# Seven block products instead of eight in half of a projection's contraction, in a two-layer attention trunk on one core

## The chip, the cores and the metric

One core of one Trainium2 chip. The metric is device time in microseconds (us) of one execution; lower is better. Engines are named as in the profile: PE (matrix products), DVE (VectorE), ACT (ScalarE), POOL (GpSimd) and SP (SyncE, which issues all the DMAs here).

## The reference

Two layers run one after the other on x of 256 tokens by 2048 features, all in float32: layer A (latent attention) and layer B (differential attention). The change touches layer B's input projection, `z = rms_norm(x, norm_g) @ w_in`, which is cut to this:

```python
z = rms_norm(x, norm_g) @ w_in                    # (256, 2048) @ (2048, 8192)
q, k, v, gate = split(z)                          # 2048 columns each, 8 heads
q = rms_norm(q.reshape(b, s, 8, 2, 128), q_gain)  # two maps a head; k likewise
o = diff_attend(q, k, v, pos, lam)                # softmax map 1 - lam * softmax map 2, times v (256 wide)
return x + (rms_norm(o, subln_g) * c * silu(gate)) @ w_out
```

## The kernel before

**Split products.** Each float32 operand of a product is split into a high part `hi` (rounded to the PE's format) and a low part `lo = x - hi`. `mm3` (L122 to L125) then makes one product of three matmuls: hi·hi, hi·lo, lo·hi. Weights are streamed: `stream` (L105) loads a chunk of 128 partitions x 1024 float32 (512 KB) into `raw` (four buffers), ACT writes `whi` (L118) and DVE writes `wlo` (L119), each of which has three buffers. A chunk holds two contraction tiles (`kk`) of 128 rows, each 512 columns wide.

**Layer B.** Each of the 8 heads has 1024 columns of the projection: a block of 512 for q and k (`wB[2h]`, summed in the two PSUM banks `pg`, one for each half `t` of the tokens) and a block of 512 for v and gate (`wB[2h+1]`, banks `pu`). `project` (L127) goes through the 8 chunks of a block: 8 x 2 `kk` x 2 `t` x 3 = 96 matmuls of 512 columns, so 192 a head. The loop over heads (L745 to L758) interleaves the attention steps of head h between pieces of these projections: `qk_t` (transposes of q and k), `soft_b` (scores and softmax), `p_b`, `av_b`, `go_b`. After the qk block, `qk_b` squares it on ACT, POOL takes the reciprocal root (`fb`, L92), and DVE multiplies from PSUM into `qk` (L641). `vg_b` splits v from PSUM (`vhb`, `vlb`) and makes the gate `sgb` (L668, L669).

**What sets the order.** Every engine has one queue in order; the tile library adds the waits and places instructions by a schedule of its own. SP's queue holds all loads. A tile with one buffer can be written again only after its last reader.

Of the kernel before, what the change touches and what calls it, by code (L numbers as in the profile page):

```python
# [51 lines left out]


@with_exitstack
def hybrid_kernel(ctx: ExitStack, tc: tile.TileContext, x, xT, pos, posc, rows, gains, wz, wgA, wqu, wkvu, woA, wB, woB, out):
# [105 lines left out]
    sqx = sm.tile([P, 2 * S], F32, tag="kn", name="sqx", bufs=1)  # L161
    XC = [0, 1] + list(range(2, KD + 1, 2))
    for k in range(KD):
        def load_x(k=k):
            n = XC[XC.index(k) + 1] - k
            xs = att.tile([P, n, S], F32, tag="gT", name="xs", padded_shape=[P, 4, S])
            nc.sync.dma_start(xs, xT[:, k:k + n, :])
            if k == 0:
                nc.sync.dma_start(gains_t, gains)
            xt[0] = (k, xs, n)  # L170

        if k in XC and k > 0:
            load_x()
        wh, wl = stream(wz[k], ZW, [c for c, _ in ZB] + [ZW] if k < KCUT else None, load_x if k == 0 else None)
        k0, xs, n = xt[0]
        split_gain(xh[:, k, :], xl[:, k, :], xs[:, k - k0, :], gA_t[:, k:k + 1])
        for b, (c0, w) in enumerate(ZB):
            for t in range(NT):
                sl = slice(t * P, (t + 1) * P)
                mm3(zacc[b][t][:, :w], xh[:, k, sl], xl[:, k, sl], wh[:, c0:c0 + w], wl[:, c0:c0 + w],  # L180
                    k == 0, k == KD - 1)
        if k == k0 + n - 1:
            w = n * S
            if k < 2:
                A.activation(sqx[:, k * S:(k + 1) * S], xs.rearrange("p a b -> p (a b)"), AF.Square)
            else:
                sq = sm.tile([P, w], F32, tag="sg", name="sq", bufs=2)
                A.activation(sq, xs.rearrange("p a b -> p (a b)"), AF.Square)
                G.tensor_tensor(sqx[:, :w], sqx[:, :w], sq, ALU.add)
# [46 lines left out]
    cs = sm.tile([P, 2, NT, HR], F32, tag="cs", name="cs", bufs=1)  # L236
# [9 lines left out]
    ropc = const.tile([P, 2, NT, ROPE], F32, tag="ropc", name="ropc")  # L246
    rops = const.tile([P, 2, NT, ROPE], F32, tag="rops", name="rops")
# [20 lines left out]
    maskA = const.tile([P, NT, S], F32, tag="maskA", name="maskA")  # L268
# [8 lines left out]
    # lambda, on every partition  # L277
# [8 lines left out]
    m16 = big.tile([P, 2, 2, 4, S], F32R, tag="m16", name="m16")  # L286
    krope = const.tile([P, NT, ROPE], F32, tag="krope", name="krope")
# [4 lines left out]
    def latents():  # L292
# [13 lines left out]
        for t in range(NT):  # L306
            cn = att.tile([P, 2, LORA], F32, tag="gT", name="cn")
# [86 lines left out]
    def q_up(hp):  # L394
        """queries of two heads, not scaled: their norm enters with the scores"""
# [4 lines left out]
        r2 = sm.tile([P, NT, 2, ROPE], F32, tag="r2", name="r2", bufs=1)  # L400
# [21 lines left out]
    def head_t(hp):  # L422
# [179 lines left out]
    def mm_b(i, pool, c0, c1):  # L602
        if c0 == 0:
            state["acc", i] = pair(pool)
        project([state["acc", i]], lhs1, [wB[i]], 512, c0, c1, KD)
        if c1 == KC:
            return state.pop(("acc", i))

    mm_b(0, psg, 0, 2)
# [17 lines left out]
    def qk_b(h, c0, c1):  # L627
        acc = mm_b(2 * h, psg, c0, c1)
        if not acc:
            return  # L630
# [9 lines left out]
        for t in range(NT):  # L640
            V.tensor_tensor(qk[:, t], acc[t].rearrange("p (j d) -> p j d", j=4), bc(f[:, t], HD), ALU.mult)  # L641
# [16 lines left out]
    def vg_b(h, c0, c1):  # L658
        acc = mm_b(2 * h + 1, psu, c0, c1)
        if not acc:  # L660
            return
# [77 lines left out]
    def out_b(n, pool, c0, c1):  # L739
        if c0 == 0:  # L740
            oacc[n] = pair(pool)
        project([oacc[n]], feat(goh2, gol2), [woB[n]], 512, c0, c1, KD)

    qk_b(0, 2, KC)
    for h in range(BH):  # L745
        vg_b(h, 0, 3)
        qk_t(h)
        vg_b(h, 3, 5)
        soft_b(h)
        vg_b(h, 5, 7)  # L750
        p_b(h)
        vg_b(h, 7, KC)
        nxt = (lambda a, b: qk_b(h + 1, a, b)) if h + 1 < BH else (lambda a, b: out_b(0, psg, a, b))
        nxt(0, 2)
        av_b(h)
        nxt(2, 5)
        go_b(h)
        nxt(5, KC if h + 1 < BH else 7)  # L758

# [22 lines left out]
def _columns(w, width):  # L782
    """(K, N) -> (N / width, K / 256, 128, 2 * width): blocks of columns in chunks of two row tiles."""
# [49 lines left out]
```

## Time and profile before

| | |
|---|---|
| median of 3 runs (lowest to highest) | 847.49 us (846.46 to 847.53) |
| span of the profiled execution | 845.0 us |
| PE, DVE, ACT, POOL busy | 99%, 67%, 58%, 10% of the span |
| bytes read from HBM | 145.73 MB |
| period of a head of layer B | 48.3 us |

The time of the profiled execution itself is not listed apart from its span; the median of the three runs is 2.5 us above that span, and these 2.5 us lie around the span (start and end of the program). The profile's views are of this one execution. In them a line such as L119 is a line of the kernel above; a row of the timeline gives start and duration in us.

### The profile page before, as it was taken

Reading aid. Unit: us, or ns where it says so; the run is one execution under the profiler, and the core shown is the slowest. Engines: PE = TensorE matmul, PEld = TensorE weight load, DVE = VectorE, ACT = ScalarE, POOL = GpSimd, SP = SyncE. Lnnn points to the kernel's source line nnn. Section 1 sums busy time; section 2 is a strip of 40 time slices with the busy share of each in tenths; the row PEclk is TensorE's granted clock in tenths of the full one; section 3 lists DMA queues with packets and bytes.
Section 4 is the critical chain, followed back from the end, with each engine's and each line's share of the span. In section 5 each row is a group of like instructions: output and inputs, shape, how many; then the busy total and the mean of one; then the engine's idle time right before and its main releaser. Section 6 shows DMA issues by size and latency. Waiting matters only on the chain.

```text
span 845.0 us, 11706 instructions
## 1 busy us (share of the span) xinstructions
PE 835.9 (99%) x4187; PEld 714.5 (85%) x4187; DVE 564.6 (67%) x968; ACT 488.0 (58%) x995; POOL 86.4 (10%) x113
## 2 busy tenths in 40 slices
PE   8999999999999999999999999999999999999998
PEld 6988888889888888888888888888888888888886
DVE  6968678788787866555647565565756566565543
ACT  7656687677767656555555465555555564554331
POOL 2300221122202200000010010010001000000000
PEclk9999999999999999999999999999999999999999
DMA  8755544534444645555555555554555555455661
GB/s 268 256 197 162 166 147 146 176 116 162 144 144 149 248 154 180 180 186 177 185 175 174 175 175 175 175 175 150 193 181 175 175 175 171 168 184 198 219 211 70
DMA packets 42954, 148.59 MB, mean 176 GB/s; under 512 B 5008, under 2 KB 6032, under 8 KB 42640
## 3 DMA queue, kind: packets, MB, share of 16 engines
q1 hardware_dynamic: 42896, 147.84, 52.5%
q8 instruction: 33, 0.54, 0.3%
q14 instruction: 25, 0.20, 0.1%
HBM read 145.73 MB, written 2.10 MB: 175 GB/s over the span
## 4 chain that ended last, share of the span: by engine, by line
PE 94%; DVE 3%; DMA 1%; ACT 1%; issue 0%; SPq 0%; POOL 0%; DVEq 0%; ACTq 0%
PE pu L123 14%; PE pu L125 14%; PE pu L124 14%; PE pg L124 13%; PE pg L123 13%; PE pg L125 13%; DVE wlo L119 1%; PE ptb L651 1%; PE ptn L430 1%; PE ptp L484 1%; PE pa L124 1%; DMA raw<-in_wz 1%; PE pa L125 1%; PE pa L123 1%; DVE xl L152 1%; PE ps L462 0%
## 5 line engine op out<-in xcount | busy, mean ns | idle before, releaser
L119 DVE TENSOR_TENSOR wlo<-raw,whi 128x1024 fp32r<-128x1024 f32 (+4 forms) x278 | 328.6, 1191 | 189.8 <-ACT whi L118 189.5
L118 ACT CAST whi<-raw 128x1024 fp32r<-128x1024 f32 (+3 forms) x277 | 282.2, 1025 | 233.6 <-PE pg L125 102.6
L123 PE MATMUL pu<-whi,x1h 128*128 128x512 f32 x256 | 101.3, 396 | 0.0
L123 PE MATMUL pg<-whi,x1h 128*128 128x512 f32 x256 | 100.5, 392 | 0.0
L125 PE MATMUL pu<-whi,x1l 128*128 128x512 f32 x256 | 99.9, 390 | 0.0
L124 PE MATMUL pu<-wlo,x1h 128*128 128x512 f32 x256 | 99.8, 390 | 0.0
L124 PE MATMUL pg<-wlo,x1h 128*128 128x512 f32 x256 | 99.7, 390 | 0.0
L125 PE MATMUL pg<-whi,x1l 128*128 128x512 f32 x256 | 99.7, 389 | 0.0
L125 PEld LDWEIGHTS pu<-whi,x1l 128*128 128x128 f32 x256 | 48.1, 188 | 10.2
L125 PEld LDWEIGHTS pg<-whi,x1l 128*128 128x128 f32 x256 | 48.1, 188 | 10.1
L123 PEld LDWEIGHTS pg<-whi,x1h 128*128 128x128 f32 x256 | 48.1, 188 | 9.5
L124 PEld LDWEIGHTS pg<-wlo,x1h 128*128 128x128 f32 x256 | 48.1, 188 | 9.4
L124 PEld LDWEIGHTS pu<-wlo,x1h 128*128 128x128 f32 x256 | 48.2, 188 | 9.2
L123 PEld LDWEIGHTS pu<-whi,x1h 128*128 128x128 f32 x256 | 48.1, 188 | 9.2
L123 PE MATMUL pg<-whi,xh 128*128 128x512 f32 (+1 forms) x128 | 49.8, 391 | 1.9 <-ACT whi L118 1.3
L124 PE MATMUL pg<-wlo,xh 128*128 128x512 f32 (+1 forms) x128 | 48.7, 381 | 1.9 <-DVE wlo L119 1.9
L123 PE MATMUL pg<-whi,goh 128*128 128x512 f32 x128 | 50.5, 395 | 0.0
L123 PE MATMUL pu<-whi,goh 128*128 128x512 f32 x128 | 50.1, 392 | 0.0
L124 PE MATMUL pg<-wlo,goh 128*128 128x512 f32 x128 | 49.9, 390 | 0.0
L125 PE MATMUL pg<-whi,gol 128*128 128x512 f32 x128 | 49.9, 390 | 0.0
L124 PE MATMUL pu<-wlo,goh 128*128 128x512 f32 x128 | 49.9, 390 | 0.0
L125 PE MATMUL pu<-whi,gol 128*128 128x512 f32 x128 | 49.9, 389 | 0.0
(246 smaller groups left out, 1551.1 us busy)
## 6 DMA issues: line engine op xcount, KB each, us to landing
raw<-in_wB SPq DMA_DIRECT2D x128, 512.0 KB, 3.2
raw<-in_wgA SPq DMA_DIRECT2D x32, 512.0 KB, 3.5
raw<-in_woA SPq DMA_DIRECT2D x32, 512.0 KB, 3.3
raw<-in_woB SPq DMA_DIRECT2D x32, 512.0 KB, 3.2
raw<-in_wkvu SPq DMA_DIRECT2D x16, 512.0 KB, 4.3
raw<-in_wz SPq DMA_DIRECT2D x15, 544.0 KB, 5.7
raw<-in_wqu SPq DMA_DIRECT2D x16, 384.0 KB, 3.1
x<-in_x SPq DMA_DIRECT2D x1, 2048.0 KB, 10.0
```

What stands on the lines that cost most here:

```text
L118: (V.tensor_copy if after_first and a == 0 else A.copy)(hi[:, a:b], raw[:, a:b])
L119: V.tensor_tensor(lo[:, a:b], raw[:, a:b], f32(hi[:, a:b]), ALU.subtract)
L123: T.matmul(o, shi, mhi, start=start, stop=False)
L124: T.matmul(o, shi, mlo, start=False, stop=False)
L125: T.matmul(o, slo, mhi, start=False, stop=stop)
L152: V.scalar_tensor_tensor(lo, src, g, f32(hi), ALU.mult, ALU.subtract)
L430: T.transpose(pt[:, h, t * P:(t + 1) * P], src[:, t, h, :NOPE], ident)
L484: T.transpose(pt[:, c, t * P:(t + 1) * P], e[:, t, c * P:(c + 1) * P], ident)
L651: T.transpose(pt[:, m, t * P:(t + 1) * P], qk[:, t, 2 * i + m, :], ident)
```

## The change

For the chunks 0 to 3 (`FAST = 4`) of each head, the two token halves x two `kk` tiles on one side and the two `kk` tiles x two column blocks on the other are taken as 2x2 block matrices, and the four block products are made by seven products in Winograd's form. Chunks 4 to 7 stay as they were (`eight`). Two chunks make a group g (`GROUPS = 2`). The sums of activation blocks (`sums`, on POOL, split into `sh` and `sl`) are made once; the sums of weight blocks `t1` to `t4` are made anew for each head and group, on POOL but for one on DVE, and each is split like a loaded chunk (`form`: `fhi` on ACT, `flo` on DVE). Each `product` is 2 chunks x 3 = 6 matmuls. `rows` loads one `kk` half of two chunks (512 KB in pieces of 2 KB instead of 4 KB); the half `b22` is loaded twice. The first four products stand in four PSUM banks, which `join` combines into an SBUF tile `d` of four quarters; the other three products and chunks 4 to 7 are summed in four banks more, which `quarters` adds to `d`. From `d` `qk_b` and `vg_b` now read; the multiplication into `qk` moves from DVE to POOL. The attention steps of head h - 1 stand between the pieces of head h.

```diff
+FAST = 4
+GROUPS = FAST // 2
...
+    def sums(c, pt):
...
+        G.tensor_tensor(s[:, 0], x10, x11, ALU.add)
+        G.tensor_tensor(s[:, 2], x00, x10, ALU.subtract)
+        G.tensor_tensor(s[:, 1], s[:, 0], x00, ALU.subtract)
+        G.tensor_tensor(s[:, 3], x01, s[:, 1], ALU.subtract)
+        split(sh[:, c], sl_[:, c], s)
...
+    def product(o, lhs, g, src, start, stop):
+        hi, lo = form(src)
+        for j in range(2):
+            c = 2 * g + j
+            sl = slice(j * 512, (j + 1) * 512)
+            mm3(o, *lhs(c), hi[:, sl], lo[:, sl], start and c == 0, stop and c == FAST - 1)
+
+    def seven_1(h, g):
+        b11 = rows(2 * h, g, 0)
+        b12 = rows(2 * h + 1, g, 0)
+        b22 = rows(2 * h + 1, g, 1)
+        t1, t2, t3 = t_tile("t1"), t_tile("t2", GROUPS), t_tile("t3")
+        G.tensor_tensor(t1, b12, b11, ALU.subtract)
+        (V if g % 2 else G).tensor_tensor(t3, b22, b12, ALU.subtract)
+        G.tensor_tensor(t2, b22, t1, ALU.subtract)
...
+        todo = [(c11, own(0, 0), b11), (c21, summed(2), t3), (c12, summed(0), t1), (c22, summed(1), t2)]
+        if g == GROUPS - 1:
+            todo = [todo[3], todo[2], todo[0], todo[1]]
+        for o, lhs, src in todo:
+            product(o, lhs, g, src, True, True)
+
+    def join(h):
+        p1, p5, p7, p6 = state["acc", h]
+        d = lb.tile([P, 4, 512], F32, tag="d", name="d")
+        A.copy(d[:, 0], p1)
+        V.tensor_tensor(d[:, 3], p6, d[:, 0], ALU.add)
+        V.tensor_tensor(d[:, 1], p5, d[:, 3], ALU.add)
+        V.tensor_tensor(d[:, 2], p7, d[:, 3], ALU.add)
+        V.tensor_tensor(d[:, 3], p5, d[:, 2], ALU.add)
...
+    def quarters(h):
...
+        for i in (1, 3, 0, 2):
+            V.tensor_tensor(d[:, i], acc[i], d[:, i], ALU.add)
+
+    def seven_2(h, g):
+        b21 = rows(2 * h, g, 1)
+        b22 = rows(2 * h + 1, g, 1)
+        t4 = t_tile("t4")
+        G.tensor_tensor(t4, b21, state.pop(("t2", h, g)), ALU.subtract)
+        c11, c12, c21, c22 = state["acc", h]
+        product(c11, own(0, 1), g, b21, True, False)
+        product(c12, summed(3), g, b22, True, False)
+        product(c21, own(1, 1), g, t4, True, False)
...
-            V.tensor_tensor(qk[:, t], acc[t].rearrange("p (j d) -> p j d", j=4), bc(f[:, t], HD), ALU.mult)
+            G.tensor_tensor(qk[:, t], acc[t].rearrange("p (j d) -> p j d", j=4), bc(f[:, t], HD), ALU.mult)
...
-    qk_b(0, 2, KC)
+    steps = [qk_t, soft_b, p_b, av_b, go_b]
     for h in range(BH):
...
+        if h > 0:
+            seven_1(h, 0)
+        for g in range(1, GROUPS):
+            seven_1(h, g)
+        join(h)
+        rest = [lambda g=g: seven_2(h, g) for g in range(GROUPS)] + [lambda c=c: eight(h, c) for c in range(FAST, KC)]
+        for n, step in enumerate(rest):
+            step()
+            if h > 0 and n < len(steps):
+                steps[n](h - 1)
+        c = quarters(h)
+        vg_b(h, c[1::2])
+        qk_b(h, c[0::2])
+    out_b(0, 0, 1)
+    for n, step in enumerate(steps):
+        step(BH - 1)
+        if n < 4:
+            out_b(0, 1 + n, 2 + n)
+    out_b(0, 5, 7)
```

Tiles that only layer A uses move to a pool that is closed before layer B; PSUM in layer B becomes six banks `pp` and two for the attention steps.

How the instructions stand on the engines now is shown in one head in the middle. In these rows L numbers of the changed kernel are the changed file's, and a number behind a tile's name tells instances apart.

POOL's queue before, one head: the softmax's bias, then the root for the sub-norm (`fo`), then the root for q and k (`fb`).

```order
L675 TENSOR_SCALAR bias_5936<-distB_653 128x512
L92 TENSOR_TENSOR fo_5267<-sso_5261,nhalf_86 128x2
L92 TENSOR_TENSOR fb_5391<-ssb_5390,nhalf_86 128x8
```

POOL's queue after, one head. `t3_5815`, `t2_5814`, `t4_5929` belong to group 0, `t1_5869`, `t2_5870`, `t4_5983` to group 1 of this head; `fb_5790` and `qk_5791` to the head before. `rows_5925` is `b21` of group 0.

```order
L671 TENSOR_TENSOR t1_5813<-rows_5809,rows_5807 128x1024
L672 TENSOR_TENSOR t3_5815<-rows_5811,rows_5809 128x1024
L673 TENSOR_TENSOR t2_5814<-rows_5811,t1_5813 128x1024
L707 TENSOR_TENSOR t4_5929<-rows_5925,t2_5814 128x1024
L671 TENSOR_TENSOR t1_5869<-rows_5865,rows_5863 128x1024
L98 TENSOR_TENSOR fb_5790<-ssb_5789,nhalf_89 128x8
L673 TENSOR_TENSOR t2_5870<-rows_5867,t1_5869 128x1024
L752 TENSOR_TENSOR qk_5791<-d_5451,fb_5790 128x512 x2
L707 TENSOR_TENSOR t4_5983<-rows_5979,t2_5870 128x1024
```

Seven sums of 1024 columns and the two multiplications into `qk` were added, and `t4` of group 0 stands ahead of `t1` of group 1. SP's queue of the same head, from `b22` of group 0 on: group 1's `b11`, `b12`, `b22`, then `b21` of group 0.

```order
L645 DMA rows_5811<-in_wB 128x2x512
L645 DMA rows_5863<-in_wB 128x2x512
L645 DMA rows_5865<-in_wB 128x2x512
L645 DMA rows_5867<-in_wB 128x2x512
L645 DMA rows_5925<-in_wB 128x2x512
```

`b21` of group 0, which POOL wants before group 1's `t1`, is asked for behind all three loads of group 1. DVE's queue at the same place, with the lows of group 0's `t1` (`flo_5844`) and `t2` (`flo_5854`):

```order
L749 TENSOR_SCALAR ssb_5789<-ssb_5789,c1x_4102 128x4
L672 TENSOR_TENSOR t3_5871<-rows_5867,rows_5865 128x1024
L158 SCALAR_TENSOR_TENSOR vlb_5779<-d_5451,r1x_4094,vhb_5778 128x256 x2
L777 SCALAR_TENSOR_TENSOR sgb_5780<-sgb_5780,d_5451 128x256 x2
L162 TENSOR_TENSOR flo_5844<-t1_5813,fhi_5843 128x1024
```

Group 1's `t3` and the head before's `vlb` and `sgb` stand ahead of group 0's `flo_5844`. PE's queue before, around the transposes of q and k:

```order
L125 MATMUL pu<-whi,x1l 128x512
L651 MATMUL ptb<-ident,qk 128x128 x8
L123 MATMUL pu<-whi,x1h 128x512
```

PE's queue after, at the end of group 0's fourth product:

```order
L131 MATMUL pp<-fhi,sl 128x512
L762 MATMUL ptb<-ident,qk 128x128 x4
L129 MATMUL pp<-fhi,sh 128x512
L762 MATMUL ptb<-ident,qk 128x128 x4
L129 MATMUL pp<-fhi,sh 128x512
L130 MATMUL pp<-flo,sh 128x512
```

The transposes of the head before's `qk` now stand behind 24 matmuls of the new head (group 0) and ahead of group 1.

More of the change, by code (lines that the diff above doesn't have):

```diff
@@ L600, in hybrid_kernel, with quad @@
     lhs1 = feat(x1h, x1l)
[L602 to L609, printed above, removed]
+    banks_a.close()
+    pp = ctx.enter_context(tc.tile_pool(name="pp", bufs=6, space=PSUM))
+    patt = ctx.enter_context(tc.tile_pool(name="patb", bufs=2, space=PSUM))
+    def quad():
+        return [pp.tile([P, 512], F32, tag="pp", name="pp") for _ in range(4)]
@@ new lines, in form, with rows @@
+    def form(src):
+        hi = wp.tile([P, 1024], F32R, tag="whi", name="fhi", padded_shape=[P, WCH])
+        lo = wp.tile([P, 1024], F32R, tag="wlo", name="flo", padded_shape=[P, WCH])
+        split(hi, lo, src)
+        return hi, lo
+    def rows(i, g, kk):
+        raw = wp.tile([P, 1024], F32, tag="raw", name="rows", bufs=4, padded_shape=[P, WCH])
+        nc.sync.dma_start(raw.rearrange("p (c n) -> p c n", c=2),
+                          wB[i, 2 * g:2 * g + 2, :, kk * 512:(kk + 1) * 512].rearrange("c p n -> p c n"))
+        return raw
@@ new lines, in t_tile, with own, summed @@
+    def t_tile(tag, bufs=1):
+        return lb.tile([P, 1024], F32, tag=tag, name=tag, bufs=bufs)
+    def own(t, kk):
+        return lambda c: tuple(a[:, 2 * c + kk, t * P:(t + 1) * P] for a in (x1h, x1l))
+    def summed(i):
+        return lambda c: (sh[:, c, i], sl_[:, c, i])
+    def product(o, lhs, g, src, start, stop):
+        hi, lo = form(src)
+        for j in range(2):
+            c = 2 * g + j
+            sl = slice(j * 512, (j + 1) * 512)
+            mm3(o, *lhs(c), hi[:, sl], lo[:, sl], start and c == 0, stop and c == FAST - 1)
@@ new lines, in join @@
+    def join(h):
[6 more added lines that the diff above has]
+        V.tensor_tensor(d[:, 3], p5, d[:, 2], ALU.add)
+        state["d", h] = d
+        state["acc", h] = quad()
+    def quarters(h):
+        d = state.pop(("d", h))
+        acc = state.pop(("acc", h))
+        for i in (1, 3, 0, 2):
+            V.tensor_tensor(d[:, i], acc[i], d[:, i], ALU.add)
+        return [d[:, i] for i in range(4)]
@@ new lines, in seven_2, with eight @@
+    def seven_2(h, g):
[3 more added lines that the diff above has]
+        G.tensor_tensor(t4, b21, state.pop(("t2", h, g)), ALU.subtract)
+        c11, c12, c21, c22 = state["acc", h]
+        product(c11, own(0, 1), g, b21, True, False)
+        product(c12, summed(3), g, b22, True, False)
+        product(c21, own(1, 1), g, t4, True, False)
+    def eight(h, c):
+        c11, c12, c21, c22 = state["acc", h]
+        for i, acc in enumerate(([c11, c21], [c12, c22])):
+            hi, lo = stream(wB[2 * h + i][c], 1024)
+            for kk in range(2):
+                sl = slice(kk * 512, (kk + 1) * 512)
+                for t in range(NT):
+                    mm3(acc[t], *lhs1(2 * c + kk, t), hi[:, sl], lo[:, sl],
+                        i == t == 1 and c == FAST and kk == 0, c == KC - 1 and kk == 1)
@@ L624, in hybrid_kernel, with qk_b @@
     V.tensor_scalar(c1x, m1, HD * EPS, None, ALU.mult)
[L627 to L630, printed above, removed]
+    def qk_b(h, acc):
         ss = sm.tile([P, NT, 4], F32, tag="ssq", name="ssb")
@@ L656, in qk_t, with vg_b @@
         state["qkb", h] = tiles
[L658 to L661, printed above, removed]
+    def vg_b(h, acc):
         vh = att.tile([P, NT, BV], F32R, tag="vh", name="vhb")
@@ L737, in hybrid_kernel, with out_b @@
     oacc = {}
-    def out_b(n, pool, c0, c1):
+    def out_b(n, c0, c1):
         if c0 == 0:
-            oacc[n] = pair(pool)
+            oacc[n] = [pp.tile([P, 512], F32, tag="pp", name="po") for _ in range(NT)]
         project([oacc[n]], feat(goh2, gol2), [woB[n]], 512, c0, c1, KD)
-    qk_b(0, 2, KC)
+    steps = [qk_t, soft_b, p_b, av_b, go_b]
     for h in range(BH):
[L746 to L758, printed above, removed]
+        if h > 0:
[17 more added lines that the diff above has]
+    out_b(0, 5, 7)
     def finish_b(n, t, c0, c1):
```

70 lines of the change are left out of this document (43 added, 27 removed).

## The prediction

> **What bounds the kernel now.** I read the page first: the engines' shares and the chain that ended last.
>
> ```profile
> span 845.0 us, 11706 instructions
> PE 835.9 (99%) x4187; PEld 714.5 (85%) x4187; DVE 564.6 (67%) x968; ACT 488.0 (58%) x995; POOL 86.4 (10%) x113
> PEclk9999999999999999999999999999999999999999
> PE 94%; DVE 3%; DMA 1%; ACT 1%; issue 0%; SPq 0%; POOL 0%; DVEq 0%; ACTq 0%
> ```
>
> PE is busy throughout at full clock and is 94% of the chain, so a matmul that goes away is worth its issue time, as long as nothing else becomes late. Next come the stage that is changed (windows of one head: length, then each engine's busy time) and the row that shows how often a head comes round.
>
> ```profile
> 441.50:489.79 48.29, 48.29 (x234) 40.54 (x233) 29.87 (x47) 26.54 (x54) 3.80 (x4) 1.00 0.52 174
> L92 POOL TENSOR_TENSOR fb<-ssb,nhalf x8: 1637/1642/1644, 393.2 to 731.3; 128x8 f32<-128x8 f32 x8
> ACT whi L118 <- PE pg L125: 50.4, 30, 1.8
> ```
>
> A head takes (731.3 - 393.2) / 7 = 48.3 us, with DVE busy 29.9, ACT 26.5 and POOL 3.8 of it. The third row (waits in six heads) says that ACT waits for PE to free the buffers of the split weights: PE is the one that is waited for. Issue times of PE, from the timeline:
>
> ```profile
> 620.13 0.39 PE L123 MATMUL pg<-whi,x1h 128*128 128x512 f32 x1
> 621.49 0.39 PE L123 MATMUL pg<-whi,x1h 128*128 128x512 f32 x1
> ```
>
> Six matmuls start in these 1.36 us: 0.227 us each, and 1.36 us is also what one new `product` gives PE to do. A head's 192 projection matmuls are 43.5 us, so the attention steps are 48.3 - 43.5 = 4.8 us.
>
> **What is removed.** Four chunks x 24 matmuls become seven products x 2 groups x 6: 96 to 84. 12 x 0.227 = 2.7 us a head, 21.8 us in all, if PE stays the bound; a head would be 45.6 us.
>
> **What is added on ACT and DVE.** Durations of one (groups of instructions by shape, 500 to 800 us):
>
> ```profile
> L119 DVE TENSOR_TENSOR wlo<-raw,whi 128x1024 fp32r<-128x1024 f32 x101 | 123.3, 1225 | 86.3 <-ACT whi L118 86.3
> L118 ACT CAST whi<-raw 128x1024 fp32r<-128x1024 f32 x100 | 105.0, 1050 | 115.7 <-PE pu L125 54.1 <-PE pg L125 52.0 <-ACT eb L688 5.7
> L641 DVE TENSOR_TENSOR qk<-pg,fb 128x512 f32<-128x512 f32 x10 | 6.4, 686 | 8.8 <-POOL fb L92 8.8
> L152 DVE SCALAR_TENSOR_TENSOR vlb<-pu,r1x,vhb 128x256 fp32r<-128x256 f32 x12 | 5.8, 484 | 1.7 <-ACT vhb L151 1.2
> L669 DVE SCALAR_TENSOR_TENSOR sgb<-sgb,pu 128x256 f32<-128x256 f32 x12 | 4.9, 412 | 0.0
> ```
>
> Splits go from 16 to 14 + 8 = 22 a head: 6 x 1.05 = 6.3 us more on ACT, 6 x 1.23 = 7.4 on DVE. DVE also gets one `t3` (1.2) and eight additions from PSUM (as L641, 8 x 0.69 = 5.5), and loses two L641 (1.4): 29.9 + 12.7 = 42.6 us of 45.6. ACT stands at 33. By sums over a head both would still fit. But each product feeds PE for 1.36 us only, against 2.72 for a chunk, and needs 1.23 of DVE; three buffers of split weights let DVE run ahead by some 4 us, so the fast half has no slack to lose.
>
> **What is added on POOL, and its collision with DVE.** The trace of before has no sum of 1024 columns on POOL. The nearest rows, undisturbed, and then beside DVE (start, duration; in brackets the engine's idle time before):
>
> ```profile
> 122.81 0.74 POOL L416 TENSOR_TENSOR rt<-rt,r 128x256 f32<-128x256 f32 x1
> 12.24 1.28 POOL L189 TENSOR_TENSOR sqx<-sqx,sq 128x512 f32<-128x512 f32 x1 [10.95 <-ACT sq L188]
> 31.58 2.44 POOL L189 TENSOR_TENSOR sqx<-sqx,sq 128x512 f32<-128x512 f32 x1 [3.94 <-ACT sq L188]
> 31.58 1.28 DVE L119 TENSOR_TENSOR wlo<-raw,whi 128x1088 fp32r<-128x1088 f32 x1
> 32.78 1.91 DVE L152 SCALAR_TENSOR_TENSOR xl<-xs,gains_t,xh 128x256 fp32r<-128x256 f32 x2
> 454.71 1.46 POOL L675 TENSOR_SCALAR bias<-distB 128x512 f32<-128x512 f32 x1 [11.57 <-DVE mxb L686]
> 311.40 0.63 POOL L675 TENSOR_SCALAR bias<-distB 128x512 f32<-128x512 f32 x1 [24.44 <-DVE go L499]
> 454.47 1.22 DVE L119 TENSOR_TENSOR wlo<-raw,whi 128x1024 fp32r<-128x1024 f32 x1
> 122.10 0.69 DVE L156 TENSOR_TENSOR pl<-ptp,ph 128x512 fp32r<-128x512 f32 x1
> ```
>
> 256 columns more cost 0.54 us, so 1024 columns take 1.28 + 2 x 0.54 = 2.36 us. Bounds: not below 2 x (1.28 - 0.2) = 2.2 (twice the longest, without its start), not above 4 x 0.74 = 3.0; I take 2.36, on the line through both rows. One multiplication into `qk` (512 columns) is 1.28.
>
> The other rows show that POOL and DVE exclude each other where DVE reads two operands from SBUF. The sum at 31.58 took 2.44: DVE's 1.28 first, then 1.16 of its own. Then two `xl` of 0.48 took 1.91: they waited for POOL. `bias` took 1.46 instead of 0.63 where a `wlo` was running. `pl`, with one operand from PSUM, kept its 0.69. Of the new work, all `flo`, `t3`, and now `vlb` and `sgb` too (they read `d` instead of PSUM) have two SBUF operands, and all of POOL's sums read SBUF. So nearly each of POOL's sums will wait for a `flo` (about 1.1 us once the start is hidden), and the other way round.
>
> The Trainium skill ("GPSIMD Engine Reference", 3.1 Elementwise) has 4497 ns for a POOL sum of 2048 columns; half of it, an estimate, is 2.25 us. With that my sum would be about 5 x 0.11 x 8 = 4 us lower; I keep the rows' 2.36.
>
> **The chain in one head.** Loads, from issue to landing (the page's median, then minimum, median and maximum in six heads):
>
> ```profile
> raw<-in_wB SPq DMA_DIRECT2D x128, 512.0 KB, 3.2
> DMA to landing us min/median/max: 3.1/3.2/5.2
> ```
>
> Let 0 be the end of the head before on PE. POOL gets `b22` of group 0 only when the low of that head's seventh stream has freed a buffer, which needs PE to have ended stream four: 4 x 2.72 + 1.9 (attention) = 12.8 before 0, plus 1.05 + 1.23 for that split, plus 3.2 of load: -7.3. `t3` and `t2` (2 x 2.36, each behind one `flo`, 1.1) then end at about 0. From there:
>
> 1. SP asks for group 1's `b22` (its buffer is freed by `t2`) and, queued behind, for group 0's `b21`: they land at 3.2 and, as a pair, 5.0. POOL's next is `t4` of group 0: 5.0 to 7.5.
> 2. DVE's `t3` of group 1 waits for that `b22`: 3.2 to 4.4. Behind it `vlb` x2 (to 5.2), `sgb` x2, which wait for POOL's `t4` (to 8.1), then the low of `t1`, done at 9.3, and of `t2`, 10.5. PE, which had two products (2.7 us) ready, waits about 6 us and ends group 0 at 11.7.
> 3. POOL's `t1` of group 1 needs `t1`'s only buffer, free at 9.3, and the port, free at 10.5: done 12.8. `fb` 1.64: 14.4. `t2` 2.36: 16.8. `qk`, 2 x 1.28 and one `flo` between: 20.2.
> 4. PE can transpose `qk` only then, and group 1 stands behind the transposes: 20.6, with 24 matmuls (5.4 us) done. That is 15 us of waiting.
> 5. The rest of the head on PE: 60 + 96 matmuls, 35.4; attention without these transposes (0.9), 3.9; and about 2 for the ten products left, which need 10 x 1.23 + 4 x 0.69 + 1.5 of DVE, plus a POOL sum, against 15 us of PE.
>
> Period: 20.6 + 35.4 + 3.9 + 2 = 61.9, so +13.6 a head; seven heads +95. The first head has no transposes, `fb` or `qk` in its way (4.2 shorter), but its fast half starts with the same loads and sums: it waits till the low of group 1's `t2`, at 16.4 + 2.3 = 18.7, with 6.3 of PE's work done (`x1_t(3)`'s transposes among it): 12.4 + 2 - 2.7 = +11.7. At the end the last head's chain (quarters 2.7, squares about 1, `fb` 1.64, `qk` 2.56, before its transposes) has one output chunk (2.72) for cover: +5. Sum: +112.
>
> Nothing: the 16 new activation sums on POOL (layer A's output projection covers them), ACT's share (33 of 62 us), the pools' moves.
>
> **The clock.** The last matmul, the stretch behind the span's work with its granted clock, and the seven warm-up matmuls:
>
> ```profile
> 840.70 0.39 PE L125 MATMUL pu<-whi,gol 128*128 128x512 f32 x1
> 842.00:845.00 3.00, 0.00 (x0) 0.00 (x0) 0.00 (x0) 0.00 (x0) 0.00 (x0) 0.94 0.27 91
> 1.17 3.17 PE L99 MATMUL warm<-wsrc 128*128 128x512 bf16 x7 [1.17 <-DVE ones L202]
> ```
>
> Some 3.5 us after the last matmul the clock falls (0.94 over the last 3 us: half for 0.4). At the start seven matmuls of 512 columns took 3.17, about 0.43 each, twice 0.227. In point 4 PE stands from 11.7 to 18, long enough. If it then needs about 3.5 us to get the clock back, eight or nine matmuls are 0.2 us longer, some of it hidden by DVE: between 0 and 1.8, I take 1 us a head: +7.
>
> The Trainium skill ("TensorE: Matmul & The Clock Gate", Part 1) says that the clock halves after at least one idle window of about 3.4 us, free-running, and needs a busy one to return. The trace's 3.5 us agrees; what it would make of this kernel is the rival of the clock, below.
>
> All together 847.5 + 112 + 7 = 966 us.
>
> **The rivals.**
> - *Everything hidden, faster.* POOL's and DVE's work fits beside PE (42.6 and about 27 us of 45.6): 847.5 - 21.8 + 5 = 831. For it speaks that the sums over a head fit. Against: POOL's queue must get from `t2` to `qk` within the 5.4 us of group 0, and it holds four sums or multiplications of at least 1.28 and a load of 3.2. It decides if `qk` is ready by 5.4. Chance 0.03.
> - *Only the shared port counts.* If queues ran far enough ahead, a head would take the port's total: DVE's 22 x 1.07 + 3.5, POOL's 7 x 2.3 + 2.4 + 2 = 47.5 us, near the old 48.3: about 850. Against it: buffers of one `t1` and four `raw`. Chance 0.03.
> - *No exclusion for these shapes.* Points 2 to 4 lose `sgb`'s wait (2.1), `t1`'s (1.2), `qk`'s (1.1), and `t3` and `t2` end about 2 earlier: 6 us a head, 966 - 48 = 918. Chance 0.09.
> - *The clock stays low.* If the 6 us of point 2 count as idle too, PE is at half speed over most of the fast part: 40 to 60 matmuls x 0.2, half hidden, some 5 us a head more: 1005 or above. Chance 0.07.
>
> **How the numbers follow.** The forecast's chance is 0.78, its own range 930 to 1000: the steps 1 to 5 carry errors of some 4 us a head (POOL's 2.2 to 3.0, loads in 2 KB pieces of 3.2 to 5). With the case without exclusion at the lower end: 910 to 1002. A measurement of this kernel tells about 0.2% from no change. Faster: 0.03 + 0.01; same 0.01; slower 0.95.
>
> **What would show it.** Right: a head's period near 62; PE idle about 15 us a head, before the low of group 0's `t1` and most of all before `ptb`, which waits for POOL's `qk`; POOL's sums at 2.4 to 3.5; `sgb` or `flo` stretched beside POOL; PE busy 85% or less of the span. Wrong: `ptb` without a wait, sums of 1.5 us, or a period below 50.

## The result and the profile after

The changed kernel takes 988.5 us (987.2 to 989.9, four runs) against 847.5: a ratio of 1.167, with a 95% interval of 1.165 to 1.168. It is slower by 141 us; the forecast was 119. From the page of the kernel after (span, busy time by engine, granted clock, chain):

```profile
span 986.7 us, 11923 instructions
PE 868.4 (88%) x4091; PEld 713.9 (72%) x4091; DVE 723.4 (73%) x1076; ACT 545.8 (55%) x1063; POOL 265.8 (27%) x201
PEclk9999999999999997988979979889799798899999
PE 54%; POOL 13%; DVE 11%; issue 9%; DMA 8%; ACT 4%; SPq 0%; POOLq 0%; DVEq 0%; ACTq 0%
```

PE has the 96 matmuls less (4187 to 4091), but it is busy for 88% of the span, and only 54% of the chain is its own. No engine is full: POOL, at 27%, holds 13% of the chain. So the time is set by a chain of waits across engines, and not by one full engine. The granted clock of PE was 1.00 before; now it falls in every head (row PEclk) and is 0.945 on average. The waits over the whole span (waiter, releaser, us, times, longest):

```profile
ACT fhi L161 <- POOL t L673: 87.7, 8, 11.4
PE pp L130 <- DVE flo L162: 37.4, 13, 5.3
PE ptb L762 <- POOL qk L752: 36.6, 16, 4.8
POOL t L707 <- DMA rows<-in_wB: 43.3, 8, 6.0
```

And one head of the timeline after (start, duration; in brackets the idle time before; `t` is `t1` at L671, `t3` at L672, `t2` at L673 and `t4` at L707):

```profile
552.08 2.40 POOL L671 TENSOR_TENSOR t<-rows 128x1024 f32<-128x1024 f32 x1 [0.69 <-DMA rows<-in_wB]
746.42 2.40 POOL L671 TENSOR_TENSOR t<-rows 128x1024 f32<-128x1024 f32 x1 [0.85 <-DMA rows<-in_wB]
...
622.09 3.39 POOL L673 TENSOR_TENSOR t<-rows,t 128x1024 f32<-128x1024 f32 x1
629.50 1.23 DVE L672 TENSOR_TENSOR t<-rows 128x1024 f32<-128x1024 f32 x1 [1.59 <-DMA rows<-in_wB]
630.79 2.53 POOL L707 TENSOR_TENSOR t<-rows,t 128x1024 f32<-128x1024 f32 x1 [5.31 <-DMA rows<-in_wB]
630.64 2.97 DVE L158 SCALAR_TENSOR_TENSOR vlb<-d,r1x,vhb 128x256 fp32r<-128x256 f32 x2
634.20 1.22 DVE L162 TENSOR_TENSOR flo<-t,fhi 128x1024 fp32r<-128x1024 f32 x1
635.47 1.22 DVE L162 TENSOR_TENSOR flo<-t,fhi 128x1024 fp32r<-128x1024 f32 x1
635.47 0.79 PE L130 MATMUL pp<-flo,sh 128*128 128x512 f32 x1 [4.06 <-DVE flo L162]
635.55 3.37 POOL L671 TENSOR_TENSOR t<-rows 128x1024 f32<-128x1024 f32 x1 [2.23 <-DVE ssb L749]
638.87 1.64 POOL L98 TENSOR_TENSOR fb<-ssb,nhalf 128x8 f32<-128x8 f32 x1
640.48 2.34 POOL L673 TENSOR_TENSOR t<-rows,t 128x1024 f32<-128x1024 f32 x1
642.77 2.04 POOL L752 TENSOR_TENSOR qk<-d,fb 128x512 f32<-128x512 f32 x2
643.87 0.69 PE L762 MATMUL ptb<-ident,qk 128*128 128x128 f32 x2 [4.06 <-POOL qk L752]
```

The first two rows are three heads apart: (746.42 - 552.08) / 3 = 64.8 us a head, where it was 48.3. The rest is one head, from the end of `t2` of group 0 (625.48): the waits come in the forecast's order. `vlb` x2, 0.97 us of work, took 2.97 beside `t4`; `t1`, 2.40 alone, took 3.37 beside a `flo` (the low of `t2`); PE stands 4.06 us for the low of `t1` (the `flo` at 634.20) and again for `qk`.

### The profile page after: what moved, and what is told of

It reads as the page before. It is cut to its first block, busy times and chain, and to the rows that moved or that the text cites. A ratio compares the mean times of both kernels' runs of the same rounds, so it can differ in the third digit from the quotient of the medians.

```text
span 986.7 us, 11923 instructions
## 1 busy us (share of the span) xinstructions
PE 868.4 (88%) x4091; PEld 713.9 (72%) x4091; DVE 723.4 (73%) x1076; ACT 545.8 (55%) x1063; POOL 265.8 (27%) x201
## 4 chain that ended last, share of the span: by engine, by line
PE 54%; POOL 13%; DVE 11%; issue 9%; DMA 8%; ACT 4%; SPq 0%; POOLq 0%; DVEq 0%; ACTq 0%
DMA rows<-in_wB 7%; PE pp L130 5%; PE pp L129 5%; PE pp L131 5%; POOL t L673 5%; PE pu L130 4%; PE pu L131 4%; PE pu L129 4%; PE pg L130 3%; DVE flo L162 3%; PE pg L131 3%; PE pg L129 3%; PE po L131 3%; PE po L130 3%; PE po L129 3%
## 5 line engine op out<-in xcount | busy, mean ns | idle before, releaser
L125 DVE TENSOR_TENSOR wlo<-raw,whi 128x1024 fp32r<-128x1024 f32 (+3 forms) x214 | 263.4, 1241 | 111.9 <-ACT whi L124 111.6
L124 ACT CAST whi<-raw 128x1024 fp32r<-128x1024 f32 (+4 forms) x213 | 214.9, 1017 | 148.4 <-PE pp L131 71.9
L161 ACT CAST fhi<-t 128x1024 fp32r<-128x1024 f32 x64 | 66.0, 1042 | 128.4 <-POOL t L673 87.7
L162 DVE TENSOR_TENSOR flo<-t,fhi 128x1024 fp32r<-128x1024 f32 x64 | 86.8, 1368 | 61.8 <-ACT fhi L161 61.8
L130 PE MATMUL pp<-wlo,x1h 128*128 128x512 f32 x256 | 100.8, 394 | 0.3
L129 PE MATMUL pp<-whi,x1h 128*128 128x512 f32 x256 | 100.7, 398 | 0.0
L131 PE MATMUL pp<-whi,x1l 128*128 128x512 f32 x256 | 100.0, 391 | 0.0
L130 PE MATMUL pp<-flo,sh 128*128 128x512 f32 x128 | 61.8, 483 | 37.2 <-DVE flo L162 37.0
L162 DVE TENSOR_TENSOR flo<-rows,fhi 128x1024 fp32r<-128x1024 f32 x48 | 82.7, 1734 | 5.1 <-ACT fhi L161 5.1
L129 PE MATMUL pp<-fhi,sh 128*128 128x512 f32 x128 | 63.5, 496 | 24.2 <-ACT fhi L161 24.0
L707 POOL TENSOR_TENSOR t<-rows,t 128x1024 f32<-128x1024 f32 x16 | 41.0, 2560 | 144.5 <-DVE flo L162 101.2
L671 POOL TENSOR_TENSOR t<-rows 128x1024 f32<-128x1024 f32 x16 | 45.3, 2831 | 55.7 <-DMA rows<-in_wB 40.2
```

The source lines that it names most:

```text
L124: (V.tensor_copy if after_first and a == 0 else A.copy)(hi[:, a:b], raw[:, a:b])
L125: V.tensor_tensor(lo[:, a:b], raw[:, a:b], f32(hi[:, a:b]), ALU.subtract)
L129: T.matmul(o, shi, mhi, start=start, stop=False)
L130: T.matmul(o, shi, mlo, start=False, stop=False)
L131: T.matmul(o, slo, mhi, start=False, stop=stop)
L161: A.copy(hi, src)
```

## The experiments

Periods are from the first and last `fb` of a run (seven heads), which gives 63.4 for the changed kernel and 48.3 before. Where sums are on POOL, this average is lower than a head in the middle: the last `fb` has no sums of a next head in its way, and its interval is 56.4 us in the changed kernel, where the six others have a mean of 64.6. All ratios are to the kernel before, with 95% intervals.

| run | us | ratio | period |
|---|---|---|---|
| changed kernel | 988.5 | 1.167 (1.165 to 1.168) | 63.4 |
| e1 other order of sums on POOL | 946.9 | 1.117 (1.115 to 1.119) | 58.6 |
| e2 no sums | 901.4 | 1.064 (1.062 to 1.065) | 54.9 |
| e3 before + idle sums | 924.7 | 1.091 (1.090 to 1.093) | 58.2 |
| e4 `qk` on DVE | 979.5 | 1.156 (1.154 to 1.158) | 62.1 |
| e5 no sums, `qk` on DVE | 878.7 | 1.038 (1.036 to 1.039) | 51.7 |
| e6 sums and `qk` on DVE | 932.0 | 1.101 (1.099 to 1.103) | 58.0 |
| e7 a quarter of the contraction | 928.7 | 1.097 (1.095 to 1.098) | 57.0 |
| e8 before + idle products by a constant | 858.4 | 1.014 (1.012 to 1.015) | 49.7 |
| e9 best version | 859.9 | 1.015 (1.013 to 1.017) | 49.3 |
| e10 products of constants added on PE | 988.5 | 1.167 (1.164 to 1.169) | 63.5 |
| e11 one product added in the wait for `qk` | 988.7 | 1.167 (1.166 to 1.169) | 63.4 |
| e12 e3 with halved sums | 895.9 | 1.058 (1.057 to 1.060) | 54.2 |

**e1: the order on POOL.**

```diff
-        t1, t2, t3 = t_tile("t1"), t_tile("t2", GROUPS), t_tile("t3")
+        t1, t2, t3 = t_tile("t1", 2), t_tile("t2", GROUPS), t_tile("t3")
...
-        t4 = t_tile("t4")
+        t4 = t_tile("t3")
```

> The seven sums, the products and every engine's work are those of the changed kernel; only POOL's order differs. t1 gets two buffers and t4 takes t3's buffer, so t1 and t2 of group 1 stand ahead of both t4 on POOL instead of behind t4 of group 0. Theory A (the period is the chain through POOL's order, with POOL and DVE taking turns): t1(g1) loses the 2.5 us of t4 and its wait for b21 ahead of it and fb and qk come some 5 us earlier, so the head's period falls from 64.7 us to 59 to 61 and the time from 988 to 945 to 960 us. Rival B (what counts is how long POOL is busy, 24 us a head, not the order): nothing changes, 985 to 990 us. Rival C (the half clock alone costs the time and follows the split work of ACT and DVE): within 10 us of 988.

Its page (busy times) and its waits:

```profile
PE 858.6 (91%) x4091; PEld 708.4 (75%) x4091; DVE 729.5 (77%) x1076; ACT 545.5 (58%) x1063; POOL 284.2 (30%) x201
```

```profile
PE ptb L762 <- POOL qk L752: 2.9, 2, 2.4
PE pp L130 <- DVE flo L162: 46.2, 21, 5.5
```

41.6 us less, with POOL busy 18 us more than in the changed kernel: POOL's total does not set the time, its order does, with the second buffer for `t1` that allows it. The wait for `qk` is as good as gone (36.6 to 2.9); the wait for low parts stays and grows (37.4 to 46.2).

**e2: no sums.**

```diff
-        G.tensor_tensor(t1, b12, b11, ALU.subtract)   # and t3, t2, t4 likewise
+        t1, t2, t3 = b12, b22, b22                    # t4 = b21
...
```

> Leaves out the seven sums of the weights a head: the products take loaded rows in their place (the output is another one); all products, high and low parts, loads and joins stay, and POOL keeps bias, fb and the two qk. Theory A (sums on POOL in the chain, and their exclusion of DVE): 17 us of POOL work go from the head, with them most of the 64.7 - 48.3 us of the period; ACT's and DVE's other added work and qk's place on POOL stay, so 53 to 56 us a head and 890 to 915 us. Rival D (everything but the sums is hidden): 47 us a head, about 831 us. Rival C (ACT and DVE's added high and low parts bind, or the clock does): above 960 us.

Its waits:

```profile
PE pp L130 <- DVE flo L162: 5.9, 9, 0.8
PE ptb L758 <- POOL qk L748: 25.2, 16, 2.4
```

87 us of the 141 go with the sums. PE's waits for low parts nearly end (37.4 to 5.9), so DVE's and ACT's added splits are not what made them late.

**e4 and e5: `qk` back on DVE**, with the sums (e4) and without them (e5).

```diff
-            G.tensor_tensor(qk[:, t], acc[t].rearrange("p (j d) -> p j d", j=4), bc(f[:, t], HD), ALU.mult)
+            V.tensor_tensor(qk[:, t], acc[t].rearrange("p (j d) -> p j d", j=4), bc(f[:, t], HD), ALU.mult)
```

> One line of the changed kernel is undone: the two products of q, k and their norms (qk) go back from POOL to DVE. Theory A (POOL's t1 and t2 of group 1 and fb ahead of qk make PE wait): fb still stands behind t2(g1) on POOL, so only qk's own 2.0 us and part of its exclusion go: 62 to 64 us a head, 968 to 980 us. Rival F (qk's place on POOL is the cause, as the wait of ptb for qk has it, 4.8 us a time): this wait goes whole, 60 us a head and about 955 us. Rival B (POOL's busy time): 2.5 of 24 us, about 970 us, with the wait for ptb unchanged but for the name of the engine.

> Leaves out the seven sums of the weights (the output is another one) and takes the two qk products back to DVE: what is left of the change is the four products less, the splits of 1024 columns for the product's own operands, the joins and the order of the products. Theory A: without the sums, PE waits for qk on POOL 16 times for 25.2 us in all, and this goes for the most part, since DVE does qk in 0.69 instead of 1.04 to 2.02 us and takes no turn with itself: 901 - 20 to 30 = 871 to 882 us. Rival F (fb is the late link, not qk): 893 to 902 us. Rival D (the rest of the change is hidden, the four products less count whole): 831 us.

Waits of e4:

```profile
DVE qk L752 <- POOL fb L98: 28.9, 8, 4.0
PE ptb L762 <- DVE qk L752: 27.0, 11, 3.9
```

With the sums it is worth 9 us: `qk` now waits for `fb`, which stands behind `t1` of group 1 on POOL as before (not behind `t2`, as my expectation has it). That the waits table names `qk` did not mean that moving `qk` ends the wait. Without the sums it is worth 22.7. What e5 keeps of the loss, one head by windows and then the rows of PE at which it waits (a third idle stretch, 0.90 us, is for an `fhi`):

```profile
470.96:522.49 51.53, 48.38 (x221) 37.76 (x221) 41.16 (x62) 33.09 (x61) 2.98 (x3) 1.00 0.59 184
```

```profile
472.22 0.50 PE L130 MATMUL pp<-flo,sh 128*128 128x512 f32 x1 [0.76 <-DVE flo L162]
474.81 0.44 PE L758 MATMUL ptb<-ident,qk 128*128 128x128 f32 x2 [1.16 <-DVE qk L748]
```

DVE is busy for 41 us (the prediction's sum was 42.6), PE for 48.4 of 51.5 (the row counts overlapping starts as busy), at full clock. What is left of the change costs 3.4 us a head over the kernel before; as 2.7 us of products are saved, it costs some 6. By PE's waits this goes to the splits and to the path from the last product to `qk`. The joins were not taken out by themselves.

**e3, e8, e12: idle work on POOL in the kernel before.** Nobody waits for it.

```diff
...
+    def idle(h, n):
+        qk = state["idle", h].rearrange("p t j d -> p (t j d)")
+        for _ in range(n):
+            G.tensor_tensor(idle_o, qk, idle_s, ALU.subtract)                   # e3, n = 7
+            G.tensor_scalar(idle_o, qk, 0.5, 0.0, ALU.mult, ALU.add)            # e8, n = 12
+            for c in (slice(0, 512), slice(512, 1024)):                         # e12, n = 7
+                G.tensor_tensor(idle_o[:, c], qk[:, c], idle_s[:, c], ALU.subtract)
...
         soft_b(h)
+        idle(h, n)
```

All three also set `dynamic_dma_scratch_size=1024` when the program is built; e8 has this too, so it can't be worth more than e8's 11 us.

> The kernel before, with seven POOL sums of 128x1024 a head added that nobody waits for (they read the head's qk tile and write a tile that is never read). Theory A (POOL and DVE take turns when both operands lie in SBUF): 7 x 2.36 = 16.5 us a head in which DVE's wlo can't run beside them; DVE's low parts come late to PE, 8 to 11 us a head, 910 to 940 us. Theory A in its weaker form (DVE 29.9 us plus 16.5 us fit into 48.3 us, so DVE catches up before PE needs it): 850 to 865 us. Rival E (no exclusion; a sum on POOL costs others nothing): 846 to 850 us, with wlo at the length that it has in the kernel before.

> A control for the idle sums: the kernel before with twelve products of one tile of 128x1024 by a constant a head on POOL in the place of the seven sums, again waited for by nobody. bias, of this form, takes 0.72 us for 512 columns and is never stretched beside DVE, so twelve take some 17 us, as much as seven sums. Theory A (POOL and DVE take turns only where both operands lie in SBUF): 846 to 853 us. Rival I (any POOL work of 17 us a head costs as much, by turns or otherwise): 910 to 930 us.

> The idle sums once more in the kernel before, each cut into two of 512 columns: 14 a head of 1.28 us undisturbed, 17.9 us, a little more POOL work than the seven of 2.36. Theory N (it is the length of one turn that counts: in the run with seven long sums one sum and one wlo took 3.32 us together, more than the 2.72 us in which PE uses up a chunk, so DVE fell behind; in the run with products by a constant a wlo took some 2.05 us and DVE kept up): here a wlo and half a sum take about 2.5 us, under 2.72, and DVE keeps up but for the softmax steps: 855 to 885 us. Rival B (POOL's total time is what counts): 924 to 932 us. Rival I (the number of turns counts, and it doubles): above 935 us.

Of each run a burst on POOL and splits beside it on DVE (timeline), and then PE's wait for the softmax (waits in six heads). First e3:

```profile
513.38 16.59 POOL L744 TENSOR_TENSOR idle_o<-qk,idle_s 128x1024 f32<-128x1024 f32 x5 [1.47 <-DVE qk L641]
513.15 7.91 DVE L119 TENSOR_TENSOR wlo<-raw,whi 128x1024 fp32r<-128x1024 f32 x3
```

```profile
PE ptpb L703 <- DVE eb L692: 34.5, 6, 5.8
```

and behind the softmax's wait in a head of e3, by windows, with the granted clock of 0.50 after the five engines:

```profile
533.24:540.07 6.83, 4.84 (x13) 3.70 (x14) 5.47 (x5) 0.59 (x1) 2.24 (x2) 0.50 0.29 87
```

e12, the sums in halves:

```profile
505.42 24.76 POOL L745 TENSOR_TENSOR idle_o<-qk,idle_s 128x512 f32<-128x512 f32 x14 [0.80 <-DVE qk L641]
524.53 4.51 DVE L119 TENSOR_TENSOR wlo<-raw,whi 128x1024 fp32r<-128x1024 f32 x2
```

```profile
PE ptpb L703 <- DVE eb L692: 20.8, 12, 2.7
```

e8, the products by a constant:

```profile
499.40 14.76 POOL L744 TENSOR_SCALAR idle_o<-qk 128x1024 f32<-128x1024 f32 x10
511.19 4.04 DVE L119 TENSOR_TENSOR wlo<-raw,whi 128x1024 fp32r<-128x1024 f32 x2
```

```profile
PE ptpb L703 <- DVE eb L692: 5.7, 12, 0.7
```

The softmax step itself (groups by shape, 500 to 800 us), in the kernel before and then in e3, e12 and e8:

```profile
L691 DVE TENSOR_SCALAR eb<-eb,denb,lamv 128x256 f32<-128x256 f32 x12 | 4.8, 441 | 0.0
```

```profile
L691 DVE TENSOR_SCALAR eb<-eb,denb,lamv 128x256 f32<-128x256 f32 x10 | 23.5, 2390 | 0.0
```

```profile
L691 DVE TENSOR_SCALAR eb<-eb,denb,lamv 128x256 f32<-128x256 f32 x12 | 14.8, 1271 | 0.0
```

```profile
L691 DVE TENSOR_SCALAR eb<-eb,denb,lamv 128x256 f32<-128x256 f32 x12 | 12.5, 1082 | 0.0
```

Sums that nobody needs cost 78 us: the cost reaches PE through DVE, which they hold up. The same sums in halves, which is more POOL work and twice the turns, cost 49. Products by a constant cost 11, but at 1.05 us undisturbed the twelve are 12.6 us of POOL work, not the 17 that the expectation counted on, so e8 has less work as well. Between e3 and e12 what changes is the length of a turn: a sum came every 16.59 / 5 = 3.32 us, a half sum every 24.76 / 14 = 1.77, a product every 1.48. Most of the price is paid in the softmax, where PE waits behind short DVE steps in series, each of which waits for a turn: 34.5 / 6 = 5.8 of e3's 9.9 us a head, 3.5 of e12's 5.9 and 1.0 of e8's 1.4. Of the rest of e3's, 7.8 / 6 = 1.3 is PE's wait for `bl` before the scores. And the clock falls during the wait: 6.83 us a head then run at half speed, with the matmuls 0.43 us apart, which costs about 2.4 us. In e12 most heads have such a stretch (mean clock 0.976), in e8 none (0.999). My expectation had looked at the splits instead, which kept up in e12 (2.26 us each against the 2.72 of a chunk), and so its 855 to 885 was too low. In e8 the expectation that one-operand work takes no turn fell: a split beside it took 2.02 instead of 1.22 us. The prediction's own row of `bias`, one operand and 1.46 instead of 0.63 us beside a `wlo`, had shown this already.

**e6: all sums on DVE; e7: a quarter of the contraction.**

```diff
-        G.tensor_tensor(t1, b12, b11, ALU.subtract)   # e6: likewise t3, t2, t4 and qk
+        V.tensor_tensor(t1, b12, b11, ALU.subtract)
-FAST = 4                                              # e7
+FAST = 2
```

> All seven sums and the two qk go from POOL to DVE (four lines of the changed kernel; the arithmetic is the same). Each sum takes 1.23 instead of 2.4 us and nothing takes turns, but DVE's work grows to about 42.6 + 7.4 + 1.4 = 51 us a head. Theory A (POOL's slow sums and the turns are the cost, DVE becomes the next bound): the period lies at DVE's 51 plus some waits, 55 to 59 us, and 915 to 945 us. Rival G (DVE's load is already the cost in the changed kernel): 988 us or more. Rival E (only the turns cost time): DVE's own 51 us a head, about 870 us.

> The same change over a quarter of the contraction instead of half of it: one group of 2x2 blocks, so 6 products less instead of 12 a head, four sums on POOL instead of six on POOL and one on DVE, and t1 and t2 of a second group no longer ahead of fb. Theory A (the chain on POOL sets the period, t4 alone stands ahead of fb, as b21 arrives): 58 to 60 us a head, 935 to 955 us. Rival H (the cost is proportional to the sums and splits): halfway, 918 us. Rival B (POOL's busy time, 24 to 17 us a head): no proportion of its own, but PE's waits for the low parts of t1 and t2 stay and those for qk go.

Against e4, which has `qk` on DVE too, e6 gains 47.5 us: on DVE a sum is half as long, takes no turn and no longer stands ahead of `fb`; these three were not tried apart. It stays 53 us above e5, so the sums still cost there. DVE is then busy for 93.7 us of the 110 in this window, so its own work is the likely reason:

```profile
500.00:610.00 110.00, 95.88 (x428) 74.24 (x426) 93.71 (x133) 63.36 (x118) 9.40 (x6) 0.96 0.52 163
```

e7 came out below its range of 935 to 955 and 11 above "halfway"; the time does not tell these two apart. Its waits name another way for POOL's chain to hold up PE. PE waits for `qk` for 2.7 us in all, but ACT's first copy of the join waits till `qk` of the head before has read `d`, which has one buffer, and PE waits for that copy:

```profile
ACT d L688 <- POOL qk L752: 24.0, 7, 3.4
PE pp L129 <- ACT d L688: 18.5, 7, 2.7
```

**e9: the parts put together.**

```diff
-FAST = 4
+FAST = 2
-        raw = wp.tile(..., bufs=4, ...)               # whi, wlo, fhi, flo: 4 in place of the pool's 3
+        raw = wp.tile(..., bufs=5, ...)
-        G.tensor_tensor(t4, ...)                      # likewise t1, t2, t3 and the two qk
+        V.tensor_tensor(t4, ...)
```

> What the runs so far point to, put together: the change over a quarter of the contraction (6 products less a head), three sums of its four as well as the fourth and the two qk on DVE, and one buffer more for loaded weights (5) and for high and low parts (4), which the smaller change leaves room for. POOL then does bias, fb and the scale of the output alone. Theory A (the sums on POOL, their place in the order and the turns were the cost; what remains is splits and joins, which the buffers cover in part): 49 to 50.5 us a head, 846 to 860 us, so at best level with the kernel before, since only 6 x 0.227 x 8 = 10.9 us are to be had. Rival J (what stays beyond the sums, 32 us in the run without them, is a cost of the products' order and of joins, at half the contraction as at a quarter): 870 to 885 us.

At 859.9 it is the best of these versions, and still 1.5% slower than the kernel before: PE waits only for `qk` (13.5 us in eight heads) and runs at full clock (0.998), yet the period is 49.3 instead of 48.3 - 1.4. Which part of it the further buffers gave was not measured apart.

**e10 and e11: the clock.**

```diff
+                for _ in range(14):                                             # e10
+                    T.matmul(pt.rearrange("p a b -> p (a b)"), wsrc[:, :P], wsrc, start=True, stop=True)
+                T.matmul(pt_flat[:8, :256], fb_flat, distB_flat[:, :256], start=True, stop=True)   # e11
                 T.transpose(pt[:, m, t * P:(t + 1) * P], qk[:, t, 2 * i + m, :], ident)
```

> The changed kernel with 14 products of constants (into the bank that the transposes of qk then take) put before the transposes of each head from the second on, so that PE works in most of its 4.5 us wait for qk; nothing waits for them. Theory A with the clock as a cost of its own (the second stretch of 6.8 us at half clock a head follows this wait, and goes; its work is then done in half the time): 2 to 3.5 us a head less, 963 to 975 us, granted clock 0.94 to 0.95 or above in each steady head instead of 0.90. Rival K (the half clock lies beside work that waits anyway): 984 to 990 us, with the clock up. Rival L (the added products themselves delay PE, which had matmuls to do there): above 992 us.

> The changed kernel with one more product a head from the second on: 128x8 (fb) by 256 columns of a constant, into the bank that the transposes then take. It stands before the last five products of group 0 in PE's order, so these run after fb is there, within the wait for qk, and the transposes of qk stay directly behind: PE's idle 4.5 us fall into two stretches under 3 us. What is left of the prediction's miss (period 64.7 us against 61.9) lies behind the transposes. Theory M (the second stretch of 6.8 us at half clock a head delays what follows the transposes): it goes, 2 to 3.5 us a head less, 965 to 976 us, with one half-clock stretch a head in place of two. Rival K (the half clock lies beside work of ACT and DVE that takes as long anyway, and the miss is theirs): 984 to 992 us, though the clock is up.

Windows of the changed kernel (its two half-speed stretches, and PE behind the transposes; the column after POOL is the granted clock), and of e11:

```profile
632.50:639.33 6.83, 3.86 (x9) 3.09 (x10) 4.18 (x6) 0.00 (x0) 4.61 (x3) 0.50 0.00 0
642.74:649.57 6.83, 5.39 (x16) 4.19 (x17) 4.90 (x4) 4.41 (x6) 2.07 (x3) 0.50 0.30 79
646.50:693.14 46.64, 44.96 (x201) 35.56 (x200) 38.58 (x51) 26.45 (x47) 12.84 (x6) 0.97 0.53 165
```

```profile
632.01:649.08 17.07, 10.47 (x27) 6.77 (x28) 9.61 (x10) 4.32 (x5) 10.63 (x6) 0.50 0.21 61
```

Neither kernel did what it was made for: e10's added products ran earlier and six of the eight transposes moved behind group 1, and in e11 the clock did not come back between the waits. They still tell something: with a mean granted clock of 0.957 (e10), 0.945 (changed) and 0.936 (e11; 17.1 us a head at half speed in place of 13.7) the period by `t1` is 64.7, 64.8 and 64.7 us. So more or less half clock before the transposes made no difference, as it would if waits hide it. The 3.1 us of it behind them (646.50 to 649.57) stayed in e11 too (2.6), so its price was not separated.

The traces leave a second reading. Every stretch at half speed is a multiple of 3.41 us long, and from head to head such stretches begin a whole number of these 3.41 us apart: 64.85 us (19 of them) in the changed kernel (632.50, then 697.35), in e10 and in most heads of e11, 58.03 (17) in e3, e6 and e7, 54.6 (16) in most heads of e2. In e1, with a period of 59.5 in its middle heads, they alternate between 58.03 and 61.44. A period that is drawn to a multiple of this length would also come out alike in the changed kernel, e10 and e11. No run tells the two readings apart.

## Why the prediction was right, and where it was short

The direction, the mechanism and the range held: 988.5 lies in 910 to 1002, above the forecast by 22.5 us. Of the signs that it named, one failed: PE was to be busy for 85% of the span or less and is busy for 88%. Up to the transposes PE is idle for 21.02 - 10.27 = 10.8 us a head (window 625.48 to 646.50), not the 15 of point 4; matmuls at half speed count as busy there.

- *What is removed*: right, 12 matmuls a head.
- *POOL's sums, 2.36 us, and the exclusion*: right, 2.34 to 2.40 alone and up to 3.4 beside DVE. That the exclusion reaches PE is shown by e3. It is wider than "two operands from SBUF": e3's softmax step and e8 show it for instructions with one.
- *Points 1 to 4*, with 0 at 625.48: `t4` ends at 7.8 (forecast 7.5), `t3` starts at 4.0 (3.2), the low of `t2` ends at 11.2 (10.5), `t1` of group 1 at 13.4 (12.8), `fb` at 15.0 (14.4), `t2` at 17.3 (16.8), `qk` at 19.3 (20.2), the transposes at 21.0 (20.6). This last figure is in part luck: `qk` took 2.0 us instead of 3.4, as no `flo` fell between its halves, and that made up for the 0.5 to 0.8 us by which the steps before it were late. The load term was short by 0.8 us, and `vlb` met `t4` instead of `sgb`. Group 0 ends on PE at 14.3 instead of 11.7 because of half clock, without consequence, since `qk` comes later.
- *Point 5* is the term that was short: 64.8 - 21.0 = 43.8 us instead of 41.3 and 1 for the clock. Half clock for 3.07 us behind the transposes loses 3.07 x (1 - 0.227 / 0.427) = 1.4 us by the rows' spacing (0.43 us between matmuls there). Counted from start to start of PE's matmuls, the waits in this stretch are 2.4 us, not 2, and the matmuls at full clock stand 0.230 us apart instead of 0.227, another 0.5. Some 0.2 us a head remains without a name.
- *Seven heads, first head and end*: rows of PE split them. They are the last matmul of layer A, two in head 0, and the last projection matmuls of heads 0 and 7:

```profile
367.40 0.39 PE L131 MATMUL pu<-whi,gol 128*128 128x512 f32 x1
385.76 0.79 PE L129 MATMUL pp<-fhi,sh 128*128 128x512 f32 x1 [1.48 <-ACT fhi L161]
403.78 0.50 PE L130 MATMUL pp<-flo,sh 128*128 128x512 f32 x1 [1.45 <-DVE flo L162]
427.99 0.39 PE L131 MATMUL pp<-whi,x1l 128*128 128x512 f32 x1
884.57 0.39 PE L131 MATMUL pp<-whi,x1l 128*128 128x512 f32 x1
```

  Seven heads took 884.57 - 427.99 = 456.6 us where 7 x 48.3 = 338 were needed before: 118.6 more instead of 95 + 7. The first head took 427.99 - 367.40 = 60.6 us, and by the forecast's terms 56.1 (43.5 - 2.7 + 12.4 + 2, and 0.9 of transposes). Its chain kept the forecast: the first matmul on `t2` of group 1, at 385.76, starts 18.1 us behind layer A. The 42.5 us behind it were given 37.4 (156 matmuls and 2 us): half speed lasts till 390.2, and PE waits for several more high and low parts, as at 403.78. The end is 1 us over, and layer A ends 0.9 us later than before. So here, too, what the forecast had too small is what lies behind the chain.

The rivals: *everything hidden* (831) falls with e5, which is at 879 even without sums; *only the shared port* (850) with e1, the same port work 42 us faster by order; *no exclusion* (918) with e3; *the clock stays low* did not come, half speed lasts 13.7 of 64.8 us. Step by step the loss is 87 us for the sums, 22.7 for `qk` on POOL once they are gone, and 31.7 for the rest, in which the 21.8 us of saved matmuls are already counted. These shares depend on the order in which parts are taken out: `qk` alone gives 9.

## What to carry to other kernels

Before trading matmuls for element-wise sums, lay the sums into the queues and follow one period: a slow engine that is idle three quarters of the time can set the pace through its order, as a new buffer and another order (e1) were worth 42 us without removing any work. Idle work on POOL is not free where DVE feeds PE with two-operand instructions; if it must go there, short instructions hurt less than long ones (e12). And a wait names the last link alone: moving that link (e4) moved the time by 9 us, taking the work in front of it (e2) by 87.

## What the runs showed of the hardware

- POOL work with one operand takes turns with DVE as well: twelve products by a constant had a mean of 1.47 us beside DVE and 1.05 at the least, and a split 2.02 instead of 1.22. The Trainium skill ("SBUF — State Buffer", SBUF: two separate sides) says that a DVE instruction with two SBUF inputs locks out any GpSimd instruction that reads SBUF, and the other way round; e8 agrees, and my expectation there was wrong by this sentence.
- A DVE step with one tensor from SBUF was held up too: the softmax's `eb` (L691, one tensor and two columns of factors) took 0.44 us before and 2.39 beside e3's sums. The step ahead of it (L686, one operand in PSUM) kept its 0.41 us beside them.
- Half speed comes in multiples of one length: 6.83 us twice in the changed kernel, and 17.07 us in e11, in which PE worked 10.5 us. These are 2 and 5 times 3.41, and single ones of 3.41 stand in e10. Over all runs, half speed ended behind a 3.41 in which PE was busy for 2.7 us or more, and it went on behind others with up to 3.1, as in this part of e11 with 2.89:

```profile
642.25:645.66 3.41, 2.89 (x9) 1.79 (x8) 1.69 (x1) 2.77 (x3) 2.61 (x3) 0.50 0.49 137
```

  The Trainium skill ("TensorE: Matmul & The Clock Gate", Part 1) has free-running windows of 3413 ns, of which a busy one is needed to return; both lengths agree. An idle one, as the prediction quotes it, was not needed for the fall: in the changed kernel PE was busy for 0.49 us from 629.09 to 632.50, where half speed begins.
- The same 512 KB of weights took longer from issue to landing, 3.2 before and 4.0 to 4.1 after (medians of the DMA issues), in the loads of two 2 KB pieces a partition (`rows`) and in those that the change did not touch (`raw`) alike. In e7, though, `raw` stayed at 3.2 with `rows` at 3.8, so neither the pieces nor anything else is shown to be the reason.
